# Block 2 of the first feed-forward networks: from twelve plain weight chunks to seven quadrant products

## The chip, the cores and the metric

The kernel runs on one core of a Trainium2 chip. Its time is the device time in microseconds (us) of one execution; the number to predict is the median over several runs. A profiled execution of the kernel before gives the trace from which all rows below are taken.

## The reference

Two layers, each a feed-forward network (FFN), a mixer and a second FFN, on 256 rows of width 1024, all in float32:

```
def swiglu(h, w_gate, w_up, w_down):
    return (jax.nn.silu(h @ w_gate) * (h @ w_up)) @ w_down
...
    for l in range(DEPTH):
        g = norm_gains[l]
        f1 = swiglu(rmsnorm(x, g[0]), ffn_w_gate[l, 0], ffn_w_up[l, 0], ffn_w_down[l, 0])
        x = x + 0.5 * rmsnorm(f1, g[1])
        m = hybrid_mixer(rmsnorm(x, g[2]), w_in[l], ...)
        x = x + rmsnorm(m, g[3])
        f2 = swiglu(rmsnorm(x, g[4]), ffn_w_gate[l, 1], ffn_w_up[l, 1], ffn_w_down[l, 1])
        x = x + 0.5 * rmsnorm(f2, g[5])
```

The hidden width of an FFN is 2816. The mixer holds a state-space scan (S5), an attention over chunks and their gates.

## The kernel before

**Numbers in two halves.** Each float32 operand is split into a high part, a copy in the format that TensorE multiplies at full rate, and a low part, the rest. A product takes three matmuls: high by high, low by high, high by low. Weights arrive from memory as chunks of 128 x 1024 (512 KB) in a buffer of the class `raw` (12 slots). ScalarE copies such a chunk to `wh`, VectorE subtracts to get `wl` (8 slots each). A chunk gives 12 matmuls of 128 x 512: six for each of the two tiles of 128 rows (t = 0, 1).

**Added chunks.** For the chunks whose number in the layer stands in `ADDED`, VectorE is left out: ScalarE writes minus `wh` into `wl`, and a transfer issued by GpSimd adds `raw` to it (`add_to`).

**An FFN** has 66 chunks and is worked in six blocks of hidden columns, five of 512 and one of 256 (blocks 0 to 5). A plain block of 512 takes 8 chunks for gate and up and then 4 for down, with the previous block's hidden values: 144 matmuls.

**A block in quadrants** (function `seven`; the table `SEVEN` says which blocks of which FFN) makes the product of 2 x 2 quadrants, the two row tiles by the halves of the width against gate and up, with seven products in place of eight. That is 84 matmuls for gate and up instead of 96, and 48 for down as before. For that it needs sums of weight chunks: four pairs of sums over the 8 chunks. The pairs 1 and 2 are subtractions on VectorE (`raw<-raw,raw`); the pairs 3 and 4 (`BY_DMA`) are a change of sign on ScalarE and an adding transfer from GpSimd (`raw<-raw`). So the 8 chunks become 14 that have to be split into `wh` and `wl`. All eight are in `raw` slots while the sums are made. The sums of the activations (`sums`) are made once per FFN.

**Order.** Every operation is recorded into a graph with a due time; `schedule` then lists them for the engines by due time, with costs, latencies and slots that are written in the file, and each engine runs its list in that order. Operations belong to a named stream (`conv` for the splits, `prep` for the constants of the S5, `main` for the rest); where one stream feeds another, `MARGIN` says by how much earlier the feeder is due. Loads are issued by SyncE (SP) one behind the other, each when its `raw` slot is free.

**Prep.** The S5 constants of a layer are worked out during an earlier FFN: for layer 0 in its first FFN, for layer 1 from the second FFN of layer 0 on. Three of its tables are in `raw` slots from the moment that GpSimd first writes them (`MEMSET raw`) until the mixer ends, two more from its last part on. It uses VectorE (142 short instructions), ScalarE and some transposes.

**Boundaries.** Behind each FFN and mixer `boundary` scales the result and adds it to x; a power (`pow`) on GpSimd gives the scale for each row. `pre_gain` makes x times the next gain ahead of it.

Before the change blocks 1 and 3 of the first FFN of each layer are in quadrants, and blocks 1 to 4 of the second.

Of the kernel before, what the change touches and what calls it, by code (L numbers as in the profile page):

```python
# [27 lines left out]
SP_LR, SP_LI, SP_DT, SP_D, SP_B = 0, 16, 32, 48, 52  # L28

N_BLK = (512, 512, 512, 512, 512, 256)  # L30
SEVEN = (((1, 3), (1, 2, 3, 4)), ((1, 3), (1, 2, 3, 4)))
FFN_CHUNKS = 66
MIX_CHUNKS = 52
LAYER_CHUNKS = 2 * FFN_CHUNKS + MIX_CHUNKS
# [4 lines left out]
ORDERED = ("blk", "ps", "s1", "s2", "s4", "s16", "gain")  # L39
LAG = 3  # L40
TAU = 1.395
MARGIN = {"conv": 7.558, "conv0": 3.423, "task": 7.748, "att0": 37.576, "s50": 37.749, "att1": 28.585, "sums": 3.0, "s51": 29.753, "prep": 40.0}
PREP_AT = (3, 149)
BIAS_AT = 50
LOOK = 0.027
# [7 lines left out]
DMA_RATE = 350e3  # L53
ADD_LAT = 8.0
BY_DMA = ((3, 4), (3, 4))
ADDED = range(44, 66, 2)


class Buf:
# [79 lines left out]
class Graph:  # L139
# [69 lines left out]
    def schedule(self):  # L209
        for o in reversed(self.ops):  # L210
            d = 1e9
            for s in o.succ:
                m = MARGIN.get(o.stream, 0.0) if s.stream != o.stream else 0.0
                d = min(d, s.due - m - o.cost - self.latency(o, s))
# [109 lines left out]
class Kern:  # L324
# [154 lines left out]
    def weight(self, i):  # L479
        if i not in self.ws:  # L480
# [3 lines left out]
            parts = (slice(0, 512), slice(512, 1024)) if i < 2 else (slice(0, 1024),)  # L484
            self.ws[i] = self.halves(self.load(i, parts), parts, i % LAYER_CHUNKS in ADDED)
            g.stream, g.rank, g.due = keep
# [91 lines left out]
    def pre_gain(self, t, l, i):  # L578
        if l >= DEPTH:
            return None  # L580
        x, g = self.x[t], self.gain(l, i)
        out = []
        for h in range(2):
            s = slice(h * 512, (h + 1) * 512)
            a = self.blk()
            self.tt(a, x[:, s], g[:, s], ALU.mult)
            out.append(a)
        return out

    def boundary(self, t, l, i, banks, scale, eps, nl_, ni_, pre):  # L590
        x, g = self.x[t], self.gain(l, i)
        gg = self.gains(l, i, nl_, ni_) if pre else None
        ss = self.small(2)
        fg, fgg = [self.blk(), self.blk()], [None, None]
        half = [slice(0, 512), slice(512, 1024)]
        for h in range(2):
            junk = self.blk(BF16, 1024)
            self.act(junk[:, :512], banks[h], AF.Square, accum_out=ss[:, h:h + 1], scale=scale)
            if pre:
                fgg[h] = self.blk()  # L600
                self.tt(fgg[h], banks[h], gg[h], ALU.mult)
        for h in range(2):
            self.tt(fg[h], banks[h], g[:, half[h]], ALU.mult)
        rs = self.rsqrt(ss[:, 0:1], ss[:, 1:2], eps)
        xs = None
        if pre:
            for h in range(2):
                self.stt(pre[h], fgg[h], rs, pre[h])
            xs = self.to_lhs(pre)
        for h, a, b in ((0, 0, 512), (1, 0, 512)) if pre else ((0, 0, 512), (1, 0, 384), (1, 384, 512)):  # L610
            c = slice(512 * h + a, 512 * h + b)
            self.stt(x[:, c], fg[h][:, a:b], rs, x[:, c])
            if not pre:
                self.dma(self.out_d[t * P:(t + 1) * P, c], x[:, c])
        return xs, self.row_scale(t) if pre else None

    def sums(self, xs):
        self.mode("sums", "bulk")
# [116 lines left out]
    def ffn(self, l, f, normed):  # L735
# [5 lines left out]
        for b, wd in enumerate(N_BLK):  # L741
            if b in SEVEN[l][f]:
                if s is None:
# [494 lines left out]
def _one_k(w):  # L1238
    return w.reshape(-1, P, 1024)


def _ffn_chunks(g, u, d, seven):
    gu, dn = [], []
    o = 0
    for wd in N_BLK:
        s = slice(o, o + wd)
        if wd == 512:
            gu.append(np.concatenate([_two_k(g[:, s]), _two_k(u[:, s])]))
        else:
            gu.append(_two_k(np.concatenate([g[:, s], u[:, s]], axis=1)))  # L1250
        dn.append(_one_k(d[s]))
        o += wd
    out = [gu[0]]
    for i in range(1, len(N_BLK)):
        if i in seven:
            out += [gu[i][:2], dn[i - 1][:1], gu[i][2:], dn[i - 1][1:]]
        else:
            out += [gu[i], dn[i - 1]]
    out.append(dn[-1])
    return np.concatenate(out)  # L1260


def _pack(a):
    f = np.float32
    wall = []
    for l in range(DEPTH):
        w_in = a["w_in"][l]
        wall.append(_ffn_chunks(a["ffn_w_gate"][l, 0], a["ffn_w_up"][l, 0], a["ffn_w_down"][l, 0], SEVEN[l][0]))
        for blk in (0, 2, 1, 3, 6, 7, 4, 5):
# [5 lines left out]
        wall.append(_one_k(a["w_o"][l]))  # L1275
        wall.append(_ffn_chunks(a["ffn_w_gate"][l, 1], a["ffn_w_up"][l, 1], a["ffn_w_down"][l, 1], SEVEN[l][1]))
    wall = np.ascontiguousarray(np.concatenate(wall))
# [43 lines left out]
```

## Time and profile before

| what | value |
|---|---|
| median of 3 runs | 1142.31 us (1141.41 to 1143.92) |
| the profiled execution, its own time | 1140.49 us |
| its span, first to last instruction | 1138.7 us |
| TensorE (PE) busy | 1116.7 us, 98% |
| VectorE (DVE) busy | 947.4 us, 83% |
| ScalarE (ACT) busy | 752.4 us, 66% |
| GpSimd (POOL) busy | 96.8 us, 9% |

The span is the profiled execution without some 1.8 us around it. A share of busy time is an average over the whole program; a matmul's row ends later than the next one's begins, so PE's busy time hides short waits.

### The profile page before, as it was taken

To read this page: it belongs to the slowest core of one execution; us is meant where nothing else is said; L and a number is where in the kernel's file an instruction comes from. 1 tells how busy PE (TensorE), PEld (TensorE's weight loads), DVE (VectorE), ACT (ScalarE), POOL (GpSimd) and SP (SyncE) were. 2 spreads that over 40 slices of the span, in tenths; PEclk is the share of its full clock that TensorE was granted. 3 is DMA by queue.
4 is the path that set the end of the run, shared out by engine and by line. 5 is a ranking of instruction groups with operands and counts; after the bars stand their busy time and mean duration, and the time that the engine had idled before them with its cause. 6 is when DMAs were issued, how large, how long until landed. Compare 5 with 4: busy or idle time off the path is not lost.

```text
span 1138.7 us, 15993 instructions
## 1 busy us (share of the span) xinstructions
PE 1116.7 (98%) x5728; PEld 887.3 (78%) x5728; DVE 947.4 (83%) x1396; ACT 752.4 (66%) x1072; POOL 96.8 (9%) x137
## 2 busy tenths in 40 slices
PE   8999999999999999999999999999999999999997
PEld 6778777777778888777888888777777888888886
DVE  6998874796877899999899789567959688999983
ACT  7857685637754687677577567846386456887752
POOL 1101120000000020101020012200000000211000
PEclk9999999999999999999999999999999999999999
DMA  9875997535374566889749679963534655779951
GB/s 348 235 304 136 328 308 218 175 107 186 102 254 167 190 144 201 280 277 265 268 133 277 221 202 319 292 220 132 169 128 145 226 185 166 184 210 280 288 185 37
DMA packets 70351, 241.75 MB, mean 212 GB/s; under 512 B 8192, under 2 KB 8960, under 8 KB 70272
## 3 DMA queue, kind: packets, MB, share of 16 engines
q1 hardware_dynamic: 60192, 204.03, 50.3%
q0 software_dynamic: 10080, 36.70, 17.3%
q8 instruction: 45, 0.74, 0.2%
q14 instruction: 34, 0.28, 0.1%
HBM read 202.96 MB, written 1.05 MB: 179 GB/s over the span
## 4 chain that ended last, share of the span: by engine, by line
PE 74%; DVE 10%; ACT 6%; issue 5%; DMA 5%; POOL 0%; SPq 0%; DVEq 0%; POOLq 0%; ACTq 0%
PE ps L418 69%; DVE wl L378 5%; PE ps L432 3%; DMA raw<-in_wall_dram 3%; ACT blk L371 3%; ACT wh L371 2%; DVE blk L378 2%; DMA wl<-raw 2%; PE ps L424 1%; DVE raw L378 1%; DVE blk L397 1%; ACT raw L371 1%; POOL s L393 0%; SPq L354 0%; ACT L371 0%
## 5 line engine op out<-in xcount | busy, mean ns | idle before, releaser
L418 PE MATMUL ps<-wh,blk 128*128 128x512 f32 x2848 | 879.6, 400 | 5.2 <-DVE blk L378 2.2
L418 PEld LDWEIGHTS ps<-wh,blk 128*128 128x128 f32 x2848 | 530.9, 188 | 131.0 <-ACT blk L371 4.1
L371 ACT ACTIVATE wh<-raw 128x1024 fp32r<-128x1024 f32 (+1 forms) x442 | 454.7, 1052 | 253.3 <-PE ps L418 197.7
L378 DVE TENSOR_TENSOR wl<-raw,wh 128x1024 fp32r<-128x1024 f32 (+1 forms) x420 | 497.8, 1213 | 126.9 <-ACT wh L371 125.2
L418 PE MATMUL ps<-wl,blk 128*128 128x512 f32 x1424 | 525.2, 399 | 1.4 <-DVE wl L378 1.4
L418 PEld LDWEIGHTS ps<-wl,blk 128*128 128x128 f32 x1424 | 266.9, 188 | 63.5 <-DVE wl L378 4.4
L371 ACT ACTIVATE blk<-ps 128x512 fp32r<-128x512 f32 (+4 forms) x156 | 86.0, 562 | 70.7 <-PE ps L432 50.1
L378 DVE TENSOR_TENSOR blk<-ps,blk 128x512 fp32r<-128x512 f32 (+2 forms) x164 | 109.1, 670 | 13.7 <-ACT blk L371 13.4
L432 PE MATMUL ps<-ident,blk 128*128 128x128 f32 x432 | 78.4, 275 | 1.8 <-ACT raw L371 1.8
L382 POOL DMA_DIRECT2D raw<-raw x48 | 41.7, 872 | 340.7 <-ACT raw L371 265.8
L432 PEld LDWEIGHTS ps<-ident,blk 128*128 128x128 f32 x432 | 55.1, 140 | 19.4 <-ACT raw L371 2.7
L371 ACT ACTIVATE blk<-blk 32x128 f32<-32x128 f32 (+4 forms) x148 | 59.0, 399 | 15.9 <-DMA blk<-in_sp_dram 9.1
L393 POOL TENSOR_TENSOR s<-s,mhalf 128x1 f32<-128x1 f32 x24 | 24.2, 1007 | 488.9 <-DVE s L405 488.9
L378 DVE TENSOR_TENSOR raw<-raw,raw 128x1024 f32<-128x1024 f32 x48 | 58.0, 1216 | 0.1
L371 ACT ACTIVATE blk<-ps,s 128x512 f32<-128x512 f32 (+1 forms) x68 | 43.7, 655 | 20.3 <-PE ps L418 13.7
L371 ACT ACTIVATE raw<-raw 128x1024 f32<-128x1024 f32 x48 | 50.2, 1052 | 5.1 <-DVE raw L378 5.1
L378 DVE TENSOR_TENSOR blk<-blk,blk 128x512 f32<-128x512 f32 (+3 forms) x70 | 42.5, 624 | 0.1
L371 ACT ACTIVATE blk<-blk,s 128x128 f32<-128x128 f32 (+2 forms) x76 | 34.6, 485 | 7.5 <-DVE blk L378 7.4
L397 DVE SCALAR_TENSOR_TENSOR blk<-blk,s,blk 128x512 f32<-128x512 f32 x44 | 32.5, 744 | 0.9 <-ACT blk L371 0.8
L382 POOL DMA_DIRECT2D wl<-raw x22 | 19.1, 866 | 108.1 <-ACT wl L371 54.3
L378 DVE TENSOR_TENSOR blk<-ps,raw 128x512 f32<-128x512 f32 x32 | 19.8, 678 | 6.8 <-PE ps L418 6.8
L418 PEld LDWEIGHTS ps<-blk,blk 128*32 128x32 f32 (+2 forms) x256 | 15.4, 147 | 12.0 <-issue 9.8
(100 smaller groups left out, 447.1 us busy)
## 6 DMA issues: line engine op xcount, KB each, us to landing
raw<-in_wall_dram SPq DMA_DIRECT2D x366, 512.0 KB, 5.5
raw<-raw POOLq DMA_DIRECT2D x48, 512.0 KB, 5.7
wl<-raw POOLq DMA_DIRECT2D x22, 512.0 KB, 8.3
gain<-in_gains_dram SPq DMA_DIRECT2D x22, 256.0 KB, 4.4
blk<-in_bias_dram SPq DMA_DIRECT2D x8, 256.0 KB, 5.8
raw<-in_wall_dram SPq DMA_DIRECT2D x4, 256.0 KB, 3.9
blk<-in_sp_dram SPq DMA_DIRECT2D x4, 256.0 KB, 8.5
x<-in_x_dram SPq DMA_DIRECT2D x3, 256.0 KB, 5.3
```

The costliest lines, as they stand in the source:

```text
L371: self.nc.scalar.activation(out=out.ap(), in_=in_.ap(), func=func, **k)
L378: lambda: self.nc.vector.tensor_tensor(out=out.ap(), in0=a.ap(), in1=b.ap(), op=op))
L382: lambda: self.nc.gpsimd.dma_start(out=out.ap(), in_=in_.ap(), accum_op=ALU.add), func="dma")
L393: lambda: self.nc.gpsimd.tensor_tensor(out=out.ap(), in0=a.ap(), in1=b.ap(), op=ALU.pow))
L397: return self.g.op("dve", cost, [out], [a, s, b], lambda: self.nc.vector.scalar_tensor_tensor(out=out.ap(), in0=a.ap(), scalar=ap(s), in1= ...
L418: return self.g.op("pe", cost, [out], [lhsT, rhs], lambda: self.nc.tensor.matmul(out.ap(), lhsT=lhsT.ap(), rhs=rhs.ap(), start=start, stop ...
L424: self.nc.tensor.matmul(out.ap(), lhsT=lhsT.ap(), rhs=rhs.ap(), start=start, stop=stop)
L432: lambda o=o, s=s: self.nc.tensor.transpose(o.ap(), s.ap(), self.ident.ap()))
```

## The change

Three things. Block 2 of the first FFN of each layer goes through `seven`, with its sums 1 and 2 on VectorE and 3 and 4 by transfer, as in the other blocks. `ADDED` has other chunks: before 44, 46, ... 64 (eleven), after 34, 42, 44, 47, ... 65 (ten); 34 and 42 are down chunks of block 3. And the operations of `pre_gain` and `boundary` (other than the last one) get streams of their own, `pre` and `edge`, with margins of 10 and 4 us.

```
-SEVEN = (((1, 3), (1, 2, 3, 4)), ((1, 3), (1, 2, 3, 4)))
+SEVEN = (((1, 2, 3), (1, 2, 3, 4)), ((1, 2, 3), (1, 2, 3, 4)))
...
-MARGIN = {"conv": 7.558, ...
+MARGIN = {"pre": 10.0, "edge": 4.0, "conv": 7.558, ...
...
-ADDED = range(44, 66, 2)
+ADDED = (34, 42, *range(44, 66, 3))
...
     def pre_gain(self, t, l, i):
...
+        self.mode("pre", "main")
         out = []
...
+        self.mode()
         return out
...
     def boundary(self, t, l, i, banks, scale, eps, nl_, ni_, pre):
         x, g = self.x[t], self.gain(l, i)
+        self.mode("pre", "main")
         gg = self.gains(l, i, nl_, ni_) if pre else None
+        self.mode("edge" if pre else "main", "main")
...
-        return xs, self.row_scale(t) if pre else None
+        rs = self.row_scale(t) if pre else None
+        self.mode()
+        return xs, rs
```

In the program as built, by count: 24 matmuls of 128 x 512 fewer; on DVE 14 splits (`wl<-raw,wh`) and 8 sums (`raw<-raw,raw`) more, and 10 instructions of 128 x 512 more; on ACT 12 `wh<-raw` and 8 changes of sign more, and 2 `wl<-wh` fewer; on POOL 8 adding transfers into `raw` more and 2 into `wl` fewer. Half of each is in either layer.

Where block 2 of layer 0's first FFN begins, DVE's list before is a run of splits of plain chunks, and then the first short instructions of prep (`pt_...`):

```order
L378 TENSOR_TENSOR wl_680<-raw_593,wh_639 128x1024
L378 TENSOR_TENSOR wl_690<-raw_607,wh_671 128x1024
L378 TENSOR_TENSOR wl_701<-raw_624,wh_683 128x1024
L378 TENSOR_TENSOR wl_710<-raw_634,wh_695 128x1024
L378 TENSOR_TENSOR wl_721<-raw_650,wh_707 128x1024
L378 TENSOR_TENSOR wl_730<-raw_661,wh_718 128x1024
L378 TENSOR_TENSOR blk_739<-ps_506,blk_636 128x512
L405 TENSOR_SCALAR pt_en_743<-prm_415 128x16
L378 TENSOR_TENSOR pt_den_746<-prm_415 128x16
L397 SCALAR_TENSOR_TENSOR blk_739<-blk_739,s_46_233,blk_528 128x512
```

After, the same place holds block 2's sums and the splits of the sums:

```order
L378 TENSOR_TENSOR raw_579<-raw_640,raw_579 128x1024
L378 TENSOR_TENSOR wl_746<-raw_620,wh_676 128x1024
L378 TENSOR_TENSOR blk_756<-ps_731,blk_743 128x512
L378 TENSOR_TENSOR wl_761<-raw_567,wh_692 128x1024
L378 TENSOR_TENSOR wl_769<-raw_579,wh_754 128x1024
L378 TENSOR_TENSOR raw_567<-raw_655,raw_567 128x1024
L378 TENSOR_TENSOR raw_579<-raw_668,raw_579 128x1024
L378 TENSOR_TENSOR wl_798<-raw_699,wh_777 128x1024
L378 TENSOR_TENSOR wl_808<-raw_567,wh_792 128x1024
L378 TENSOR_TENSOR wl_819<-raw_579,wh_803 128x1024
```

The prep instructions have moved behind these: their first five now stand at the end of block 2's list, and the rest behind the splits of block 3.

POOL's list of adding transfers in the same FFN, before: the last two rows of block 1, the four of block 3, then the chunks of `ADDED`:

```order
L382 DMA raw_304<-raw_254 128x1024
L382 DMA raw_322<-raw_271 128x1024
L382 DMA raw_819<-raw_883 128x1024
L382 DMA raw_857<-raw_906 128x1024
L382 DMA raw_776<-raw_726 128x1024
L382 DMA raw_796<-raw_736 128x1024
L382 DMA wl_1231<-raw_1136 128x1024
L382 DMA wl_1255<-raw_1165 128x1024
```

After: block 1, block 2's four, chunk 34, block 3's four, chunk 42, and so on:

```order
L382 DMA raw_304<-raw_254 128x1024
L382 DMA raw_322<-raw_271 128x1024
L382 DMA raw_628<-raw_655 128x1024
L382 DMA raw_640<-raw_668 128x1024
L382 DMA raw_604<-raw_567 128x1024
L382 DMA raw_620<-raw_579 128x1024
L382 DMA wl_931<-raw_879 128x1024
L382 DMA raw_920<-raw_951 128x1024
L382 DMA raw_934<-raw_969 128x1024
L382 DMA raw_891<-raw_851 128x1024
L382 DMA raw_908<-raw_862 128x1024
L382 DMA wl_1126<-raw_1078 128x1024
```

Ten adding transfers now belong to blocks 2 and 3, where four did; of the chunks behind them eight are added, where eleven were.

## Rows read from the trace of the kernel before

**Rows 1.** The profile's page, part 1: busy time of each engine.

```profile
PE 1116.7 (98%) x5728; PEld 887.3 (78%) x5728; DVE 947.4 (83%) x1396; ACT 752.4 (66%) x1072; POOL 96.8 (9%) x137
```

**Rows 2.** Waits of the PE: engine, line, releaser; total us, times, longest; 20:208, 570:770.

```profile
PE ps L432 <- ACT raw L371: 1.1, 1, 1.1
PE ps L418 <- DVE blk L403: 1.1, 1, 1.1
...
PE ps L432 <- ACT raw L371: 0.7, 1, 0.7
```

**Rows 3.** Stretches: window, length, busy us (instructions) by engine, clock, DMA share, GB/s.

```profile
28.00:58.00 30.00, 30.00 (x135) 24.02 (x134) 30.00 (x34) 26.14 (x33) 3.65 (x4) 1.00 0.88 242
58.00:133.00 75.00, 73.70 (x326) 58.96 (x325) 64.44 (x143) 48.95 (x53) 6.67 (x9) 1.00 0.78 248
133.00:160.00 27.00, 27.00 (x122) 21.84 (x121) 23.85 (x62) 20.54 (x38) 6.26 (x10) 1.00 1.03 314
160.00:194.00 34.00, 32.63 (x201) 24.41 (x201) 15.42 (x18) 20.34 (x30) 3.41 (x7) 1.00 0.85 249
445.00:545.00 100.00, 97.14 (x427) 77.02 (x426) 95.72 (x101) 73.02 (x82) 10.31 (x12) 1.00 0.88 266
593.00:695.00 102.00, 102.00 (x454) 82.36 (x453) 88.83 (x139) 72.78 (x82) 9.80 (x12) 1.00 0.79 239
726.00:756.00 30.00, 29.26 (x188) 21.97 (x187) 13.24 (x17) 16.72 (x24) 3.38 (x7) 1.00 0.85 257
1007.00:1103.00 96.00, 96.00 (x428) 77.80 (x427) 95.94 (x98) 74.13 (x83) 10.39 (x12) 1.00 0.85 252
```

**Rows 4.** The chain that ended last, second FFN of layer 1: start, us, what.

```profile
1011.24 27.88 PE ps L418 x120
1039.12 0.44 PE ps L432 x4
```

**Rows 5.** Timeline of DVE in 36:135: start, us, line, operation, tiles, count.

```profile
61.37 8.03 DVE L378 TENSOR_TENSOR wl<-raw,wh 128x1024 fp32r<-128x1024 f32 x7
...
95.13 1.28 DVE L378 TENSOR_TENSOR blk<-ps,blk 128x512 fp32r<-128x512 f32 x2
```

**Rows 6.** Groups of instructions: busy us, mean ns of one, then idle before them.

```profile
L371 ACT ACTIVATE wh<-raw 128x1024 fp32r<-128x1024 f32 (+1 forms) x442 | 454.7, 1052 | 253.3 <-PE ps L418 197.7
L378 DVE TENSOR_TENSOR wl<-raw,wh 128x1024 fp32r<-128x1024 f32 (+1 forms) x420 | 497.8, 1213 | 126.9 <-ACT wh L371 125.2
```

**Rows 7.** Timeline of POOL in 0:30 and in 380:480: the tables of prep.

```profile
19.67 0.20 POOL L359 MEMSET raw<- 128x16 f32 x3
...
425.29 0.22 POOL L359 MEMSET raw<- 128x16 f32 x2 [1.66 <-DVE wl L378]
427.55 0.13 POOL L359 MEMSET raw<- 128x16 f32 x1 [2.05 <-DVE wl L378]
```

**Rows 8.** Waits of SP, which issues the loads: total us, times, longest.

```profile
SPq L354 <- DVE wl L378: 720.4, 273, 14.1
```

**Rows 9.** The chain that ended last, all: its transfers, start and us.

```profile
106.68 9.36 DMA raw<-in_wall_dram
...
165.04 8.86 DMA wl<-raw
...
457.57 7.90 DMA raw<-in_wall_dram
```

**Rows 10.** DMA queues (packets, MB, share of 16 engines) and issues (median us to landing).

```profile
q1 hardware_dynamic: 60192, 204.03, 50.3%
q0 software_dynamic: 10080, 36.70, 17.3%
...
raw<-in_wall_dram SPq DMA_DIRECT2D x366, 512.0 KB, 5.5
raw<-raw POOLq DMA_DIRECT2D x48, 512.0 KB, 5.7
wl<-raw POOLq DMA_DIRECT2D x22, 512.0 KB, 8.3
```

**Rows 11.** The power on GpSimd at the boundaries: ns min/median/max, first and last start.

```profile
L393 POOL TENSOR_TENSOR s<-s,mhalf x24: 547/551/3727, 16.0 to 1133.2; 128x1 f32<-128x1 f32 x24
```

More of the change, by code (lines that the diff above doesn't have):

```diff
@@ L41 @@
 TAU = 1.395
-MARGIN = {"conv": 7.558, "conv0": 3.423, "task": 7.748, "att0": 37.576, "s50": 37.749, "att1": 28.585, "sums": 3.0, "s51": 29.753, "prep": 40.0}
+MARGIN = {"pre": 10.0, "edge": 4.0, "conv": 7.558, "conv0": 3.423, "task": 7.748, "att0": 37.576, "s50": 37.749, "att1": 28.585, "sums": 3.0, "s51": 29.753, "prep": 40.0}
 PREP_AT = (3, 149)
```

## The prediction

> **What bounds the kernel now.** I read the page first: PE is busy for 98% of the span, DVE for 83%, ACT for 66% [rows 1]. A busy PE can still run slowly, so I looked next at what a matmul costs where nothing disturbs it. In the second FFN of layer 1 the chain is PE alone, and 120 matmuls take 27.88 us, 0.2323 each; the four transposes behind them take 0.44, 0.11 each [rows 4]. PE's clock is 1.00 of full speed in every stretch that I cite [rows 3]. So there the kernel is bound by PE, and each matmul taken away is worth its 0.2323 us.
>
> Then I asked where PE is not alone. Three blocks in quadrants, one behind the other, stand in the second FFN of both layers. In layer 1 they take 96 us with PE never idle; in layer 0 the same blocks, with as many matmuls, take 100 us with PE idle for 100 - 97.14 = 2.9 [rows 3]. DVE is busy for nearly all of both stretches, so DVE is just as fast as PE there and any stop of DVE becomes one of PE. The difference that I find between the two is in `raw` slots: in layer 0 GpSimd writes the three tables of prep at 425 to 427 us, so nine of twelve slots are left for weights from there on, while layer 1 has no prep behind it and has twelve [rows 7]. The queue of loads does wait for slots: SP waits 273 times for a split on DVE, 720 us in all [rows 8]. And the chain shows what follows in layer 0: a load that starts at 457.57 when a slot comes free and takes 7.90 us to land [rows 9]. That nine slots are the reason is my reading; the 4 us are a measurement. **The first FFN of both layers runs with nine slots**: in layer 0 the tables are written at 19.67, in layer 1 they are held since 425 [rows 7]. There the stretch of 58 to 133 us (blocks 2 and 3 of layer 0) has PE idle for 1.3, one wait of 1.1 among it, behind a load of 9.36 us at 106.68 [rows 2, 3, 9]; in layer 1, from 593 to 695, PE is not idle at all [rows 3].
>
> **The change, part by part.**
>
> *PE.* A plain block has 144 matmuls, one in quadrants 84 + 48 = 132. Two blocks: 24 x 0.2323 = 5.58 us less, on the path. Their transposes stay.
>
> *DVE.* Seven splits on DVE in a row take 8.03, the last of them with its full 1.21, so they start (8.03 - 1.21) / 6 = 1.135 apart; the second of two half-size ones starts 0.60 behind the first (1.28 - 0.68, a row's length) [rows 5, 6]. A block in quadrants has 18 splits, 4 sums and 9 of half size: 22 x 1.135 + 9 x 0.60 = 30.4 us. PE needs 132 x 0.2323 + 8 x 0.11 = 31.5 for it. So DVE fits with 1.1 to spare in a block, and no more. Over the two layers it gets 14 splits, 8 sums and 10 halves: 22 x 1.135 + 10 x 0.60 = 31 us more. Of this 15.5 falls to each first FFN. What hides it: DVE's idle time of 10.6 in 58:133, 3.2 in 133:160 and 18.6 in 160:194 [rows 3], and the order, which puts prep's short instructions behind the splits of block 3. Blocks 2 and 3 then ask 2 x 30.4 - 2 x 1.135 (chunks 34 and 42 are added) = 58.5 of DVE against 63.0 of PE. It fits, but the lead is gone: the cover that block 2 gave as a plain block was this idle time, and 28:58 shows DVE at 30.00 of 30 us when block 2 begins [rows 3].
>
> *What is late next.* With DVE level with PE and nine slots, the three blocks of layer 0's second FFN are the nearest rows: (100 - 96) / 3 = 1.3 us a block. The bounds for block 2 are 0 (593:695, nine slots, no wait) and 3.0 (the transfers, below). I take 1.3 in each layer, since the blocks now stand back to back as in those rows: 2.7 us given back. Block 3 of layer 0 pays its 1.3 today.
>
> *ACT.* Nine passes of 128 x 1024 more in each layer at 1.05 [rows 6]: 9.5 us, beside idle time of 26 us in 58:133 [rows 3]. Nothing on the path; without that cover it would be late by what exceeds it.
>
> *Transfers.* A load takes 0.503 x 1138.7 x 0.524 / 204.03 = 1.47 us of the 16 engines, an adding transfer 0.173 x 1138.7 / 70 = 2.81 [rows 10]. Block 2 goes from 17.6 to 12 x 1.47 + 4 x 2.81 = 28.9 in 31.5 us, which is still room. Block 3, with 34 and 42, asks 17.6 + 6 x 2.81 = 34.5 in 31.5: 3.0 us too much, to be met by what was loaded ahead. The blocks behind it are relieved, from eleven added chunks to eight. By the Trainium skill, DMA: Bandwidth & Descriptors, section "Issuing engines are not separate DMA queues", transfers of GpSimd and SP run on the same 16 engines. The trace agrees: where the added chunks crowd, 133:160, the share is 1.03 [rows 3].
>
> *The added chunks' own wait.* In layer 0 an adding transfer starts at 165.04 and takes 8.86 to land; the slot that it reads is wanted by prep's next table, ACT waits, and PE's transposes wait 1.1 for ACT; layer 1 has 0.7 at the same place [rows 2, 9]. PE is idle for 1.4 in 160:194 and 0.7 in 726:756 [rows 3]. After the change two of prep's tables per layer, not one, follow an added chunk in their slot, but fewer of these transfers run at once. Bounds -2.1 (both waits gone) and +2.1 (each twice); I take 0.
>
> *The two margins.* They move boundaries earlier in the lists. PE shows no boundary among its waits in layer 1's first FFN and mixer edge [rows 2], so I take 0. What hides a boundary is the other tile's matmuls.
>
> **Sum.** -5.58 + 2.7 = -2.9 us against the execution's own 1140.5 (span 1138.7): 1137.6. The median of the runs lies 1.8 above that execution, so I put the median at 1142.3 - 2.9 = 1139.4.
>
> **Rivals.**
>
> *All is hidden.* Layer 1's 593:695 speaks for it, layer 0's 58:133 against [rows 3]. -5.6, and with the added chunks' waits gone -7.7: 1136.7 to 1134.6.
>
> *Late transfers eat it.* The 3.0 us that block 3 lacks are not met in layer 0, where no lead is left: -2.9 + 3.0 = +0.1, 1142.4. For it: 28:58 has a share of 0.88 already, and the long landings in the chain [rows 3, 9]. Against it: a share of 1.03 in 133:160 left PE busy for all 27 us [rows 3].
>
> *Slower: DVE's stops stay.* Before, DVE stands idle for 10.6 us in 58:133 and this costs PE 1.3, since DVE was ahead. If these stops are late loads and not lack of work, blocks 2 and 3 take 58.5 + 10.6 = 69.1 on DVE against 63.0 on PE: 6.1 us, 4.8 more than is paid today. In both layers, the second with nothing paid today: -5.6 + 4.8 + 6.1 = +5.3, 1147.6. It decides from stops of 63.0 - 58.5 + 1.3 + 2.8 = 8.6 us in layer 0 and 7.3 in layer 1. Against it: in 445:545 DVE stopped for only 4.3 in three such blocks [rows 3].
>
> *The power at the boundary is held.* It takes 551 ns as a rule and up to 3727 [rows 11]. With DVE fuller at the end of the first FFN (15.4 of 34 us before [rows 3]), one more long one in each layer on the boundary's path would cost 3.2 each: -2.9 + 6.4 = +3.5, 1145.8. The other tile's matmuls speak against it. The Trainium skill, SBUF — State Buffer, section "SBUF: two separate sides", has such a lock: a VectorE instruction with two inputs in SBUF and a GpSimd one that reads SBUF shut each other out. The spread of the rows agrees.
>
> **How the numbers follow.** About 0.2%, 2.3 us, can be told from no change here. Forecast (-2.3 to -6) 0.44, all hidden and the added waits gone 0.08, transfers eat it 0.30, DVE's stops 0.13, the power 0.05. So faster 0.52, same 0.30, slower 0.18. The range goes from 1134.6, all hidden, to 1143.8, 1.5 above no change, which leaves out most of the two slower cases.
>
> **What would show it.** Right: 24 matmuls fewer at 0.23, DVE near 100% from block 1 to the end of block 3, prep's instructions after it, PE idle for some 1 to 3 us there, and layer 1's first FFN shorter by more than layer 0's. Transfers: a share near 1 in block 3 and DVE waiting for ACT and ACT for loads there. Wrong: PE waits of more than 3 us in either first FFN, a mixer that starts late because prep does, or a stretch that the change does not touch, such as layer 0's second FFN, moving by more than 2 us.

## The result and the profile after

The changed kernel takes 1136.03 us in the median of six executions (five of 1134.67 to 1138.58, and one of 1540.67 at a granted clock of 0.655, which the ratio leaves out), the kernel before 1141.99 in the same runs. The ratio is 0.9948, 95% interval 0.9928 to 0.9968: faster by about 6 us, where 1139.4 was predicted. The profiled execution takes 1135.77 us, its span is 1134.0, 4.7 less than before.

The page, part 1, against [rows 1], and the kinds of transfer against [rows 10]. The 24 matmuls are gone, VectorE has 28 us more, ScalarE 18.5:

```profile
PE 1108.6 (98%) x5704; PEld 884.9 (78%) x5704; DVE 975.8 (86%) x1428; ACT 770.9 (68%) x1092; POOL 110.1 (10%) x143
...
raw<-raw POOLq DMA_DIRECT2D x56, 512.0 KB, 5.3
wl<-raw POOLq DMA_DIRECT2D x20, 512.0 KB, 8.2
```

Where the time went is read by stage. A stage runs from its first matmul to the first of the next, so the stages of a kernel follow one another without a gap. Lengths in us, each worked out from two starts in the trace of one profiled execution; L0 and L1 are the layers, "blocks 1-3" and "4-5" are those of the first FFN, and "second FFN" is blocks 1 to 4 of layer 0's:

| kernel | L0 1-3 | L0 4-5 | L0 mixer | L0 second FFN | L1 1-3 | L1 4-5 | L1 mixer |
|---|---|---|---|---|---|---|---|
| before | 104.6 | 69.3 | 185.8 | 135.7 | 102.8 | 69.1 | 185.9 |
| after | 106.6 | 66.2 | 183.8 | 133.4 | 108.5 | 64.4 | 183.7 |
| e1 quadrants alone | 105.1 | 82.2 | 185.9 | 134.8 | 104.7 | 76.7 | 185.9 |
| e2 added alone | 106.2 | 67.6 | 186.0 | 135.8 | 103.6 | 68.9 | 186.0 |
| e3 margins alone | 104.1 | 68.1 | 183.7 | 135.2 | 102.7 | 67.2 | 184.0 |
| e4 no 34, 42 | 104.4 | 67.3 | 183.7 | 133.4 | 102.0 | 69.0 | 183.6 |
| e5 old added | 104.3 | 70.6 | 183.7 | 133.6 | 101.8 | 72.6 | 183.9 |
| e6 no margins | 104.7 | 76.2 | 185.8 | 134.7 | 105.2 | 72.5 | 185.8 |
| e7 no quadrants | 105.8 | 65.1 | 183.8 | 134.1 | 103.8 | 64.0 | 183.7 |
| e9 edge only | 103.6 | 69.0 | 183.7 | 134.5 | 102.7 | 68.8 | 183.8 |
| e10 pre only | 103.6 | 69.4 | 186.3 | 135.4 | 102.8 | 69.4 | 186.2 |
| e11 margins, late list | 103.6 | 64.3 | 183.7 | 136.3 | 102.8 | 64.5 | 183.6 |
| e12 no 42 | 104.2 | 64.5 | 183.8 | 133.5 | 103.2 | 66.6 | 183.7 |

The first two rows already speak against my working. The stages that lost 12 matmuls each, blocks 1 to 3, became longer by 2.0 and 5.7 us. What became shorter are stages that lost no matmul: blocks 4 and 5 (3.1 and 4.7), the mixers (2.0 and 2.2), and layer 0's second FFN (2.3).

The waits of PE in the changed kernel, 20:208 and 545:770, against [rows 2]:

```profile
PE ps L418 <- DVE blk L378: 1.8, 1, 1.8
PE ps L418 <- DMA wl<-raw: 1.7, 2, 1.0
...
PE ps L418 <- DMA wl<-raw: 4.2, 1, 4.2
PE ps L418 <- DVE blk L378: 1.6, 1, 1.6
```

The 4.2 is new, and so is the 1.7 of layer 0 for the same kind of transfer. In the chain of 620:700 the 4.2 is the adding transfer of layer 1's chunk 42:

```profile
667.97 7.32 DMA raw<-in_wall_dram
675.35 2.47 issue
677.83 9.64 DMA wl<-raw
687.51 12.66 PE ps L418 x44
```

The chunk's load lands after 7.32, ScalarE's two passes and the issue take until 677.83, the transfer issued then needs 9.64 more, and PE, which has run out of other work at 683.3, waits for it. By the Trainium skill, DMA: Bandwidth & Descriptors, section "Issuing engines are not separate DMA queues", a transfer from GpSimd gets no engines of its own beside SP's loads. The trace agrees, with a share of 1.01 to 1.05 in the windows below while this one is under way.

The wait costs more than its 4.2 us. Windows of PE around it (busy us, granted clock, DMA share, GB/s):

```profile
674.00:682.50 8.50, 8.50 (x39) 1.00 1.01 357
682.50:687.50 5.00, 0.82 (x4) 0.80 1.05 291
687.50:690.00 2.50, 2.49 (x6) 0.50 1.04 270
690.00:692.50 2.50, 2.50 (x8) 0.53 1.05 275
692.50:697.50 5.00, 5.00 (x24) 1.00 1.03 354
```

PE had been busy without a gap at 2.4 GHz. After the idle time its clock is 0.50 to 0.53, which is 1.2 GHz, for the next 5 us, and only then 1.00 again. By the clock that is another 2.5 x 0.50 + 2.5 x 0.47 = 2.4 us lost, an estimate from these two rows. No row that I read before the change had PE at less than 1.00, so my sum had no price for this.

VectorE did not become full either. Blocks 2 and 3, in both layers, against [rows 3]:

```profile
67.20:136.80 69.60, 66.96 (x288) 53.13 (x287) 61.22 (x93) 50.06 (x57) 10.18 (x12) 0.98 0.92 259
...
625.00:697.50 72.50, 66.70 (x284) 53.38 (x283) 63.42 (x94) 52.51 (x59) 9.93 (x13) 0.95 0.96 270
```

DVE stands idle for 69.60 - 61.22 = 8.4 us in layer 0 and 72.50 - 63.42 = 9.1 in layer 1. In layer 0 its waits in 60:137 and those of ACT say for what:

```profile
DVE wl L378 <- ACT wh L371: 6.8, 3, 3.2
...
ACT wh L371 <- DMA raw<-in_wall_dram: 13.2, 5, 6.0
```

The timelines of ACT and DVE, and the chain, have one of these stops:

```profile
87.29 2.02 ACT L371 ACTIVATE wh<-raw 128x1024 fp32r<-128x1024 f32 x2 [5.96 <-DMA raw<-in_wall_dram]
```

```profile
88.38 2.36 DVE L378 TENSOR_TENSOR wl<-raw,wh 128x1024 fp32r<-128x1024 f32 x2 [2.26 <-ACT wh L371]
```

```profile
82.79 6.69 DMA raw<-in_wall_dram
```

ACT stands still for 5.96 until a load lands, and DVE for 2.26 until ACT has copied it. The next load, which goes into the slot that a split of DVE frees at 82.7, takes 6.69 and lands at 89.48 only. DVE has its splits to do late, and at 91.9 PE waits 1.8 for an instruction of DVE behind them. In layer 0 the stops are late loads, not lack of work. In layer 1 only half are: of the waits of DVE in 625:697.5, 4.4 us are for ACT, whose own are for loads, and 4.5 for PE while it waits for chunk 42.

### The profile page after: what moved, and what is told of

Same layout as the page of the kernel before. It is cut to its first block, busy times and chain, and to the rows that moved or that the text cites. A ratio compares the mean times of both kernels' runs of the same rounds, so it can differ in the third digit from the quotient of the medians.

```text
span 1134.0 us, 15986 instructions
## 1 busy us (share of the span) xinstructions
PE 1108.6 (98%) x5704; PEld 884.9 (78%) x5704; DVE 975.8 (86%) x1428; ACT 770.9 (68%) x1092; POOL 110.1 (10%) x143
## 3 DMA queue, kind: packets, MB, share of 16 engines
HBM read 202.96 MB, written 1.05 MB: 180 GB/s over the span
## 4 chain that ended last, share of the span: by engine, by line
PE 64%; DVE 17%; issue 6%; ACT 6%; DMA 6%; POOL 1%; SPq 0%; DVEq 0%; POOLq 0%; ACTq 0%
PE ps L418 59%; DVE wl L378 8%; DMA raw<-in_wall_dram 5%; DVE blk L378 4%; PE ps L432 3%; ACT wh L371 2%; ACT blk L371 2%; DVE raw L378 2%; DVE blk L397 2%; PE ps L424 1%; POOL s L393 1%; ACT raw L371 1%; DMA wl<-raw 1%; DVE x L397 0%; DMA gain<-in_gains_dram 0%
## 5 line engine op out<-in xcount | busy, mean ns | idle before, releaser
L371 ACT ACTIVATE wh<-raw 128x1024 fp32r<-128x1024 f32 (+1 forms) x454 | 467.9, 1052 | 249.9 <-PE ps L418 174.3
L378 DVE TENSOR_TENSOR wl<-raw,wh 128x1024 fp32r<-128x1024 f32 (+1 forms) x434 | 514.3, 1215 | 86.6 <-ACT wh L371 85.7
L378 DVE TENSOR_TENSOR blk<-ps,blk 128x512 f32<-128x512 f32 (+2 forms) x174 | 116.3, 673 | 18.1 <-ACT blk L371 12.2
L382 POOL DMA_DIRECT2D raw<-raw x56 | 48.7, 869 | 302.9 <-ACT raw L371 210.4
L393 POOL TENSOR_TENSOR s<-s,mhalf 128x1 f32<-128x1 f32 x24 | 32.1, 1339 | 447.7 <-DVE s L405 440.8
L432 PE MATMUL ps<-ident,blk 128*128 128x128 f32 x432 | 72.9, 273 | 1.0 <-DVE blk L378 1.0
L432 PEld LDWEIGHTS ps<-ident,blk 128*128 128x128 f32 x432 | 54.0, 140 | 17.8 <-DVE blk L378 2.2
L378 DVE TENSOR_TENSOR raw<-raw,raw 128x1024 f32<-128x1024 f32 x56 | 67.7, 1218 | 0.0
L371 ACT ACTIVATE raw<-raw 128x1024 f32<-128x1024 f32 x56 | 58.4, 1052 | 5.1 <-DVE raw L378 4.6
L418 PEld LDWEIGHTS ps<-blk,raw 128*128 128x128 f32 x128 | 17.5, 191 | 6.0 <-ACT blk L371 3.6
```

The costliest lines, as they stand in the source:

```text
L371: self.nc.scalar.activation(out=out.ap(), in_=in_.ap(), func=func, **k)
L378: lambda: self.nc.vector.tensor_tensor(out=out.ap(), in0=a.ap(), in1=b.ap(), op=op))
L382: lambda: self.nc.gpsimd.dma_start(out=out.ap(), in_=in_.ap(), accum_op=ALU.add), func="dma")
L393: lambda: self.nc.gpsimd.tensor_tensor(out=out.ap(), in0=a.ap(), in1=b.ap(), op=ALU.pow))
L418: return self.g.op("pe", cost, [out], [lhsT, rhs], lambda: self.nc.tensor.matmul(out.ap(), lhsT=lhsT.ap(), rhs=rhs.ap(), start=start, stop ...
L432: lambda o=o, s=s: self.nc.tensor.transpose(o.ap(), s.ap(), self.ident.ap()))
```

## The experiments

Nothing of the computation is left out in any of them. The ratio is to the kernel before on the same chip; the last column is (ratio - 1) x 1141 us.

| kernel | quadrants in block 2 | added chunks | margins | median us | ratio, 95% interval | us to before |
|---|---|---|---|---|---|---|
| after | yes | 34, 42, 44, 47, ... 65 | both | 1136.03 | 0.9948 [0.9928, 0.9968] | -5.9 |
| e1 | yes | old | none | 1163.21 | 1.0196 [1.0176, 1.0215] | +22.4 |
| e2 | no | new | none | 1144.02 | 1.0033 [1.0021, 1.0046] | +3.8 |
| e3 | no | old | both | 1132.66 | 0.9931 [0.9916, 0.9947] | -7.9 |
| e4 | yes | 44, 47, ... 65 | both | 1132.29 | 0.9924 [0.9903, 0.9945] | -8.7 |
| e5 | yes | old | both | 1141.43 | 1.0012 [0.9999, 1.0025] | +1.4 |
| e6 | yes | new | none | 1155.60 | 1.0123 [1.0110, 1.0136] | +14.0 |
| e7 | no | new | both | 1130.23 | 0.9909 [0.9894, 0.9923] | -10.4 |
| e8 | no, three slots held | old | none | 1142.45 | 1.0013 [1.0002, 1.0025] | +1.5 |
| e9 | no | old | edge | 1134.37 | 0.9941 [0.9922, 0.9959] | -6.7 |
| e10 | no | old | pre | 1140.24 | 0.9994 [0.9981, 1.0007] | -0.7 |
| e11 | no | 44, 47, ... 65 | both | 1126.52 | 0.9882 [0.9863, 0.9901] | -13.5 |
| e12 | yes | 34, 44, 47, ... 65 | both | 1127.13 | 0.9889 [0.9872, 0.9906] | -12.7 |

**e1, the quadrants alone** (the `SEVEN` line of the change, nothing else).

```
+SEVEN = (((1, 2, 3), (1, 2, 3, 4)), ((1, 2, 3), (1, 2, 3, 4)))
 ADDED = range(44, 66, 2)
```

> Only block 2 in quadrants; the added chunks and the margins as before. Theory A, the prediction's: the quadrants are the whole gain, -5.6 us of matmuls and some 1.3 us given back in each layer, so about -3 us, with DVE waiting in blocks 2 and 3. Theory B, from the two traces: in the changed kernel the stretch of blocks 1 to 3 grew by 2.0 us in layer 0 and 5.7 us in layer 1, and the gain lies in the blocks behind, the mixers and layer 0's second FFN; then the quadrants alone, which keep eleven added chunks behind them, give -1 to +3 us. Neither chunk 34 nor 42 is added here, so the waits of PE for wl<-raw transfers in block 3 (1.7 and 4.2 us in the changed kernel) should be gone under both.

It took 22 us more, where neither expectation had a loss above 3. The loss isn't in blocks 1 to 3 (104.6 to 105.1 and 102.8 to 104.7) but behind them: blocks 4 and 5 grew by 12.9 and 7.6. PE's waits there, 135:218:

```profile
PE ps L418 <- ACT blk L371: 3.2, 1, 3.2
PE ps L432 <- ACT raw L371: 2.6, 1, 2.6
```

Prep ends on DVE at 181.5, before at 157.6, and the boundary's first product of gains begins at 183.8 in place of 166.9. What I called hidden was hidden only as far as blocks 1 to 3 go. But the 15.5 us of DVE work are not all of it, for DVE stands idle there too, for 10.3 us up to 158.56. The longest wait, 3.2, comes from a load of prep's parameters (`blk<-in_sp_dram`, 256 KB). It is issued at 143.68 and takes 12.36 us; ACT, which runs its list in order, stands in front of its copy, and DVE and, up to 158.58, PE wait behind ACT:

```profile
156.12 0.84 ACT L371 ACTIVATE blk<-blk 64x256 f32<-64x256 f32 x2 [11.24 <-DMA blk<-in_sp_dram]
```

Layer 1 has the same with 10.6 us of ACT and 2.5 of PE. The waits are not the whole loss of layer 0 either. The stage as a window of PE:

```profile
135.80:218.10 82.30, 73.14 (x361) 0.94 0.82 236
```

PE is idle for 9.2 us, 7.8 more than before; a granted clock of 0.94 in the mean is worth some 0.06 x 82.3 = 4.9 (an estimate from this row).

**e2, the new list of added chunks alone.**

```
-ADDED = range(44, 66, 2)
+ADDED = (34, 42, *range(44, 66, 3))
```

> Only the list of added chunks as in the change (34, 42 and eight of the eleven behind); block 2 plain, no margins. Theory A: nothing, within 1 us, since DVE has idle time there. Theory B: the thinner list is a gain of its own in the stretch from block 4 to the mixer (3.1 and 4.7 us shorter in the changed kernel): -2 to -4 us, with the PE waits of 1.1 and 0.7 us behind an adding transfer gone; block 3 may wait for chunk 42 as in the changed kernel.

Slower by 0.3%, so neither expectation holds, and the waits that the list was to relieve, L432 for ACT's `raw`, rose from 1.1 and 0.7 [rows 2] to 2.3 and 1.9.

**e3, the two margins alone.**

```
+MARGIN = {"pre": 10.0, "edge": 4.0, "conv": 7.558, ...
...
+        self.mode("pre", "main")
...
+        self.mode("edge" if pre else "main", "main")
```

> Only the two margins. Theory A: nothing, within 1 us: PE does not wait for a boundary. Theory B: the lists of the mixers change, where the changed kernel is 2.0 and 2.2 us shorter without a change of their work: -2 to -4 us, with the wait of 1.1 us of PE line 424 for ACT gone from both mixers.

7.9 us less than before, no less a gain than that of the whole change (5.9, the intervals overlap). The part that I had at 0 carries it. Theory B had named the place, and the wait of 1.1 is gone from both mixers, but the gain is twice what it said.

**e4, the change without the added chunks 34 and 42.**

```
-ADDED = (34, 42, *range(44, 66, 3))
+ADDED = range(44, 66, 3)
```

> The changed kernel without chunks 34 and 42 among the added ones (eight left). If the crowd of transfers in block 3 (six adding ones where 34.5 us of transfers were reckoned for 31.5 us) makes PE's waits there, the waits for wl<-raw of 1.7 and 4.2 us go, and the kernel is some 3 to 6 us faster than the changed one: -9 to -12 us against before. If DVE is what binds blocks 2 and 3, its two more splits in each layer (2.3 us) take the place of the waits, and the time stays within 2 us of the changed kernel's.

8.7 us faster than before, between the two expectations and not clear of the whole change's 5.9 (the intervals overlap). The 4.2 us wait is gone, but layer 1's blocks 4 and 5 take 69.0 in place of 64.4, with a new wait of 3.1 for DVE in them.

The next four fill the table of three parts by two settings, and test the reading on slots.

**e5, e6, e7: the change with one part taken back** (the old list; both margins at 0; block 2 plain).

```
-ADDED = (34, 42, *range(44, 66, 3))
+ADDED = range(44, 66, 2)
```

```
-MARGIN = {"pre": 10.0, "edge": 4.0, ...
+MARGIN = {"pre": 0.0, "edge": 0.0, ...
```

```
-SEVEN = (((1, 2, 3), (1, 2, 3, 4)), ((1, 2, 3), (1, 2, 3, 4)))
+SEVEN = (((1, 3), (1, 2, 3, 4)), ((1, 3), (1, 2, 3, 4)))
```

> The change with the old list of added chunks (44, 46, ... 64): quadrants and margins. The quadrants alone took 22 us more, the margins alone 8 us less. Theory M, the quadrants' loss came at the boundaries behind the first FFNs, which the margins bring forward: about 1136 us (1133 to 1140), blocks 4 and 5 to the mixer near 66 to 69 us as in the change. Theory A, it came from eleven adding transfers that meet the quadrants' DVE work, which only the thinner list takes away: about 1141 - 8 + 22 = 1155 us (1150 to 1160), and those blocks stay at 77 to 82 us.

> The change with both margins at 0: quadrants and the new list of added chunks. Theory M, the margins carry the gain and also hide the quadrants' loss: 1155 to 1165 us, slower than before by 1 to 2 per cent, and blocks 4 and 5 take 77 to 82 us. Theory A, the thinner list hides the quadrants' loss: 1138 to 1145 us, the margins' 8 us missing and nothing else. My prediction on record took the margins at nothing, so by it this kernel is at 1138.

> The change with block 2 plain as before: the margins and the new list of added chunks. If the quadrants give 2.9 us, as I predicted, this kernel takes about 1139 us. If they give nothing in the company of the margins, it takes the same as the change, 1135 to 1137 us. If they lose (blocks 1 to 3 took 2 us longer in layer 0 and 5.7 longer in layer 1), it takes 1131 to 1134 us.

The margins take away most of what the quadrants cost: e1 to e5 is 22.4 to 1.4. Of the two theories of e5 and e6, M (the margins hide it) is 1.4 us short in e5 and holds in e6 at its lower end, though the stages that it named miss by up to 4.5 us (70.6 and 72.6 in e5, 76.2 and 72.5 in e6); A (the thinner list hides it) misses e5 by 9 us and e6 by 11. The list takes away a smaller part, 22.4 to 14.0 from e1 to e6. Without the margins the waits stand behind the quadrants again. In e6, 133:210 and 700:785:

```profile
PE ps L432 <- DVE blk L378: 3.4, 1, 3.4
PE ps L418 <- ACT blk L371: 3.1, 1, 3.1
...
PE ps L432 <- DVE blk L378: 3.3, 1, 3.3
PE ps L418 <- ACT blk L371: 2.1, 1, 2.1
```

The waits for ACT, 3.1 and 2.1, again come behind the load of prep's parameters. What ACT waits for this load over the whole kernel, in the kernel before, in e1 and in e5:

```profile
ACT blk L371 <- DMA blk<-in_sp_dram: 9.1, 2, 4.9
```

```profile
ACT blk L371 <- DMA blk<-in_sp_dram: 21.8, 2, 11.2
```

```profile
ACT blk L371 <- DMA blk<-in_sp_dram: 4.6, 1, 4.6
```

It is 18.7 in e6 and 2.5 in the changed kernel, so with quadrants it is long without the margins and much shorter with them, under either list. In layer 0 of e5 the load is issued at 143.38 and its copy runs at 156.18, as in e1; but ACT's list there has splits in front of the copy (149.22 to 155.30), where in e1 they stand behind it. This part of what the margins do is shown. The waits of L432 for DVE at the boundary are another part, whose cause was not isolated.

And e7 says the most: with block 2 plain the kernel is 4.5 us faster than the change, with intervals that stay apart and 0.8 us below the lowest that I expected of quadrants that lose. In every company that I tried the quadrants of block 2 cost time: e3 to e5 +9.3, e7 to after +4.5, e11 to e4 +4.8, and without margins +22.4 and (e2 to e6) +10.2.

**e8, three slots held in the kernel before.** GpSimd writes three buffers of class `raw` before block 1 of layer 1's second FFN; they are given free behind its last loads.

```
+                if (l, f, b) == (1, 1, 1):
...
+                    held = [self.g.buf("raw", [P, 1024]) for _ in range(3)]
+                    for r in held:
+                        self.memset("pool", r[:, 0:16], 0.0, [self.g.ops[self.mark[(0, 184 + 126)]]])
...
+                    for r in held:
+                        self.act(self.small(), r[:, 0:1], AF.Copy, after=[self.g.ops[self.mark[(0, 184 + 173)]]])
```

> The kernel before, but three of the twelve raw slots are held by GpSimd in layer 1's second FFN, from about the first loads of its block 1 until its last loads, and read by ACT into small buffers that nothing uses. My reading on record was that nine slots for weights instead of twelve make layer 0's second FFN take 100 us for three blocks in quadrants where layer 1's takes 96. By it the three blocks in layer 1 (1007 to 1103 us of the span before) take 99 to 101 us, PE idles there for about 3 us on DVE or loads, and the kernel is 3 to 5 us slower. The rival, that the slots don't matter and the 4 us come from prep's instructions or the boundary: 96 us there, the time unchanged within 1 us.

Windows of blocks 2 to 4 of that FFN, first without, then with the held slots (starts shifted by what lies ahead):

```profile
1007.20:1102.50 95.30, 95.30 (x424) 77.26 (x423) 95.24 (x98) 73.88 (x82) 10.30 (x12) 1.00 0.86 254
```

```profile
1009.00:1105.80 96.80, 95.89 (x424) 76.82 (x423) 95.14 (x97) 73.44 (x85) 10.13 (x12) 1.00 0.88 266
```

The chain of this stretch, PE alone before [rows 4], now has loads in it, one of them:

```profile
1027.26 7.71 DMA raw<-in_wall_dram
```

1.5 us longer, and PE idle for 0.9. The direction of my reading is shown, with its chain; the size is not. In layer 0 the same blocks take 99.5 against layer 1's 95.3, so held slots are worth about a third of the 4.2 us, and the changed kernel with the same tables in `raw` needs only 97.4 there. What makes the rest stays open.

**e9 and e10, one margin each, in the kernel before.**

```
+MARGIN = {"pre": 0.0, "edge": 4.0, ...
```

```
+MARGIN = {"pre": 10.0, "edge": 0.0, ...
```

> The kernel before with the edge margin of 4.0 alone (pre at 0). Both margins together took 8 us less: 2 us in each mixer, 3 us in blocks 4 and 5 of the two first FFNs, the rest in small parts. Theory E, the gain is the earlier end of the boundary itself, in the mixers (a wait of PE for ACT of 1.1 us and what stands behind it): about 1134 to 1137 us, mixers 184 us long. Theory P, the gain comes from the products of x and the gains that pre brings forward, so that DVE is free when the banks are ready: 1140 to 1142 us here.

> The kernel before with the pre margin of 10.0 alone (edge at 0). Theory E: 1139 to 1142 us, mixers 186 us long as before, and the wait of 1.1 us in them stays. Theory P: 1133 to 1136 us.

Theory E holds: edge alone gives 6.7 of the 7.9, pre alone 0.7 with an interval that holds a ratio of 1. The mixers show it. The wait of PE in the kernel before, in its timeline (in brackets the idle time ahead):

```profile
270.86 1.04 PE L432 MATMUL ps<-ident,blk 128*128 128x128 f32 x4
272.99 1.57 PE L424 MATMUL ps<-blk,blk 128*64 128x128 f32 x16 [1.10 <-ACT blk L371]
```

The same place with edge alone:

```profile
272.70 0.72 PE L418 MATMUL ps<-wh,blk 128*128 128x512 f32 x2
...
274.76 1.09 PE L424 MATMUL ps<-blk,blk 128*64 128x128 f32 x16
```

Before, PE comes to the sixteen L424 with nothing else ready. With edge alone large matmuls stand in that place and no wait is left. What moved is the second tile's boundary; its row scale, the last of it on ACT, before and with edge alone:

```profile
259.76 1.06 ACT L371 ACTIVATE blk<-x 128x1024 bf16<-128x1024 f32 x1 [0.43 <-DVE x L397]
```

```profile
230.17 1.05 ACT L371 ACTIVATE blk<-x 128x1024 bf16<-128x1024 f32 x1
```

Pre alone keeps the wait of 1.1, mixers of 186 and the row scale at 259.42. The mixers give 2.1 and 2.1 of e9's 4.8 us of span; the other stages give parts of about 1 us and less, and the start takes 2 back.

**e11, margins and the late list, block 2 plain.**

```
+MARGIN = {"pre": 10.0, "edge": 4.0, "conv": 7.558, ...
+ADDED = range(44, 66, 3)
```

> The kernel before with both margins and eight added chunks (44, 47, ... 65), block 2 plain: what no_34_42 has, without its quadrants. no_34_42 took 1132.3 us. If the quadrants of block 2 give nothing even where no added chunk stands in block 3, this takes 1129 to 1132 us; if they give the 5.6 us of their matmuls there, 1137 to 1139 us; by my 2.9 us, 1135 us.

1126.52 us, with e12 the fastest of all and faster than both kernels of this study, 2.5 us under the lowest that I expected. Compared with e4 it is the cleanest test of the quadrants: the same list, the same margins, 24 matmuls more, 4.8 us less. Blocks 1 to 3 are even (103.6 against 104.4, and 102.8 against 102.0), where 2.8 us each should have been saved, and blocks 4 and 5 take 64.3 against 67.3 and 64.5 against 69.0. Windows of layer 0, blocks 1 to 3 and 4 to 5, of e11:

```profile
29.40:133.00 103.60, 103.16 (x456) 82.58 (x455) 93.93 (x163) 73.49 (x82) 9.57 (x11) 1.00 0.81 246
133.00:197.30 64.30, 64.13 (x361) 51.70 (x361) 49.41 (x106) 44.49 (x74) 9.24 (x18) 1.00 0.87 268
```

and of e4:

```profile
30.90:135.30 104.40, 101.43 (x444) 80.22 (x443) 100.99 (x129) 81.70 (x93) 13.09 (x15) 1.00 0.87 257
135.30:202.60 67.30, 64.74 (x360) 51.50 (x359) 55.40 (x156) 45.09 (x75) 9.22 (x18) 1.00 0.86 266
```

With quadrants PE has less to do and is idle for 3.0 us; then DVE has 6 us more to do in blocks 4 and 5, and PE waits there for 2.6. Plain, DVE has idle time left in blocks 1 to 3 (9.7 us) and prep is done in it.

**e12, the change without the added chunk 42.**

```
-ADDED = (34, 42, *range(44, 66, 3))
+ADDED = (34, *range(44, 66, 3))
```

> The changed kernel with chunk 42 loaded plainly, chunk 34 still added. In the changed kernel PE waited 4.2 us in layer 1 for chunk 42's adding transfer, and its next matmuls ran for about 5 us at a lower clock. Theory T, that one transfer is the cost: about 6 us less in layer 1's blocks 1 to 3 (102 to 103 us instead of 108.5), 1129 to 1132 us in all. Theory C, block 3 has too many transfers and the wait moves to another load: 1134 to 1137 us, and a wait of PE for a transfer of over 2 us elsewhere in that stretch.

Theory T holds: one chunk of the list takes the gain from 5.9 to 12.7, 6.8 us by the ratios, where it said about 6. (The medians, 1136.03 and 1127.13, are of two chips and differ by more.) Layer 1's blocks 1 to 3 go from 108.5 to 103.2, PE waits no more for a transfer there, and this is all that is left of its waits (585:700):

```profile
PE ps L418 <- DVE blk L378: 2.6, 2, 1.5
```

PE's idle time in that stage fell from 5.8 to 2.6, and with the granted clock at 1.00 the 2.4 us of the lower clock are gone too: 5.6, where 5.3 are measured. Blocks 4 and 5 behind it took 2.2 us longer, with a wait of 1.9 for DVE. Chunk 34 on the other hand rather helps: e4 to e12 is -8.7 to -12.7, with intervals that just overlap.

## Why the number was right and the working was not

**PE, 24 matmuls at 0.2323.** The count is right, the saving is not seen. Blocks 1 to 3 should have become 2.8 shorter in each layer and became 2.0 and 5.7 longer. In place of 2.7 us, 4.8 and 8.5 were given back, 13.3 in all. Of the 4.8, 2.3 are idle time of PE (3.6 in the stage, 1.3 before) and 1.7 the lower clock behind the wait at 91.9; of the 8.5, 5.8 are idle time and 2.4 the clock.

**"I take 1.3 in each layer"** is the first step that failed. I took the three quadrant blocks of layer 0's second FFN as the nearest rows, where DVE is nearly level with PE, and read their loss as one of slots. There DVE has hardly any prep to do and no chunk is added. Here both come on top: late loads (behind most of DVE's 8.4 us of idle time in layer 0 and half of its 9.1 in layer 1), one adding transfer (4.2), and the clock (1.7 and 2.4). The rival "DVE's stops stay" came nearest to this stretch. It was to decide from stops of 8.6 us in layer 0 and 7.3 in layer 1, and its price by stage, -2.8 + 4.8 = +2.0 and -2.8 + 6.1 = +3.3, stands beside +2.0 and +5.7; what layer 1 has above it is chunk 42, which the rival did not have. I gave it 0.13.

**Transfers.** Bounded by 3.0 us for block 3, in layer 0. There they came due with 0.7 (a second wait, of 1.0, stands in block 4), and in layer 1 as one wait of 4.2 for chunk 42. A share of the engines summed over a block says nothing of when a single chunk lands; the list put the chunk's transfer where the share was already 1.01.

**DVE, +31 us, hidden by idle time and by prep moved behind.** Measured 28.4. (6.82 / 6 is 1.137 and not 1.135, which changes no sum.) What e1, e4 and e6 show is that the prep which moved behind is not free: it stands in front of the boundary, and ACT's copy of its parameters stands in front of splits while the load of these parameters is still under way. My sum had no term for that load. The margins lessen both: for the load ACT's list shows how, for the boundary it is shown by comparison only.

**"The two margins ... I take 0"** is the step that failed most, by 7.9 us alone and by 20 to 21 in the company of the quadrants (e6 to after, e1 to e5). The reason that I gave, no boundary among PE's waits, was read from windows that ended at 208 and 770, some 5 us behind the mixers' first matmuls. The second tile's boundary lies inside the mixer, and the wait of 1.1 before 272.99 stood one window further on.

**The added chunks' own wait.** Taken at 0 between -2.1 and +2.1. Blocks 4 and 5 gave 3.1 and 4.7, and what helps there is not only a wait, for the small matmuls of prep took less of PE; see the last section.

**The power.** One now takes up to 5471 ns, as the rows of L393 have it, against 3727 [rows 11]:

```profile
L393 POOL TENSOR_TENSOR s<-s,mhalf x24: 549/555/5471, 16.3 to 1128.5; 128x1 f32<-128x1 f32 x24
```

No wait of PE of that size stands at a boundary, so this rival did not come.

By the stages of the two profiled executions, the 4.7 us are made of +7.7 in blocks 1 to 3, where my whole -2.9 should have been, and of -7.8 in blocks 4 and 5, -4.2 in the mixers and -2.3 in layer 0's second FFN, all of which I had at 0; the rest, +1.9, is mostly the start, 30.2 for 28.6. The start is the clock: in 23.40:26.70 it is 0.50 in the changed kernel's trace and 1.00 in the other (rows in the last section), some 1.7 us. Which part of the change has to do with it, if any, is open: in single executions e2 and e3 have it, e8, e10 and e11 have not. The predicted number was near because errors of opposite sign met, which is luck. Of the signs that I named, DVE near 100% and a layer 1 shorter by more than layer 0 did not come; two of those for "wrong" did, a wait of PE above 3 us in a first FFN and layer 0's second FFN moving by more than 2.

## What to carry to other kernels

Split a change of several parts before believing its sum: here two margins alone gave as much as the whole, and the part that the change is named after cost 4.5 us and more in every mix. Matmuls saved in a stage are worth their time only where the engine that feeds PE keeps its cover; count what is pushed behind that stage, and look at the wait rows beyond the edge of the stage, up to the last instruction that the moved work feeds. Place each adding transfer by when its chunk is wanted, not by the sum of the transfers: taking one of ten out was worth about 7 us. And where an engine runs its list in order, ask of each instruction that waits for a load what stands behind it.

## What had not been expected of the hardware

A wait of PE can have a tail. After 4.2 us of idle time the granted clock was 0.50 to 0.53 (1.2 GHz) for 5 us; after the wait of 1.8 at 91.9 it was 0.63 in 94.3:97.0 and 0.86 in 97.0:102.0, by which 2.7 x 0.37 + 5.0 x 0.14 = 1.7 us are lost. Windows of the changed kernel:

```profile
91.90:94.30 2.40, 0.63 (x4) 1.00 1.02 418
94.30:97.00 2.70, 2.70 (x8) 0.63 1.03 416
97.00:102.00 5.00, 5.00 (x22) 0.86 0.89 252
```

It does not follow each wait. Both kernels have a wait of 1.8 for ACT at the start, at some 20 to 22 us. Behind it the clock fell in the one trace and not in the other, before and then after:

```profile
23.40:26.70 3.30, 3.30 (x14) 1.00 1.03 408
```

```profile
23.40:26.70 3.30, 3.30 (x9) 0.50 1.05 416
```

In e6 a wait of 3.35 before 750.82 left it at 1.00. So a wait cost what its row says or, in these rows, 1.7 to 2.4 us more.

Small matmuls are dear when they lie between large ones. Prep has 128 of 128 x 32. In the kernel before they lie between large ones and transposes, and their rows cover 5.5 us of PE; in the changed kernel and in e11 they stand together and cover 1.5 (the groups by shape, before and then e11):

```profile
L418 PE MATMUL ps<-blk,blk 128*32 128x32 f32 x128 | 5.5, 206 | 0.0
```

```profile
L418 PE MATMUL ps<-blk,blk 128*32 128x32 f32 x128 | 1.5, 199 | 0.0
```

The rows overlap their neighbours', so the starts say more. In e11 the 64 of layer 0 take 0.70 us up to the next large one, which starts at 182.28; in the kernel before, one large one between two runs of them takes 0.43 (183.78 to 184.21), where it takes 0.23 among its like:

```profile
181.58 0.76 PE L418 MATMUL ps<-blk,blk 128*32 128x32 f32 x64
```

```profile
183.78 0.50 PE L418 MATMUL ps<-wh,blk 128*128 128x512 f32 x1
184.21 0.31 PE L418 MATMUL ps<-blk,blk 128*32 128x32 f32 x10
```

It is the list of added chunks that decides this: every kernel with the old list has 4.6 or 5.5, those with a thinner one 1.5 to 2.4. No wait shows this time, since PE counts as busy. It is a part of why blocks 4 and 5 could gain more than the idle time that PE had in them before, 1.4 and 1.1 us.
